# A three-pass float32 encoder layer: the two parts of h side by side for the up projection, and another order for its first and last products

## The chip, the cores and the metric

The kernel runs on one core of a Trainium2 chip. The metric is the device time of one execution in microseconds, as the median of several runs. One more execution was recorded by the profiler; every row in this text comes from that one. The engines are TensorE (PE; PEld is its weight load), VectorE (DVE), ScalarE (ACT), GpSimd (POOL) and SyncE (SP), which only issues DMAs.

## The reference, cut to what matters

One layer, 512 tokens by 2048 channels, float32: an attention and pooling part, then a gated feed-forward part with a convolution over three tokens between its two projections. The change is in the first projection of the second part.

```python
def reference(x, ...):
    ...                                             # attention, pooling, w_o, residual
    h = rms_norm(x, pre_ffn_g[l])                   # (512, 2048)
    up = causal_dwconv(h @ w_up[l], conv_w[l], conv_b[l])          # w_up: 2048 x 11264
    y = (gelu(up[..., :D_FF]) * up[..., D_FF:]) @ w_down[l]        # w_down: 5632 x 2048
    x = x + rms_norm(y, post_ffn_g[l])
    return x
```

## The kernel before

**Two parts for each number.** Every factor is split into a rounded high part and the low rest, by `split`: ACT writes the high part (line 136 or 139) and DVE the low one (line 137 or 140). A plain product is then three matmuls (`mm3`, lines 152 to 154): high by high, high by low, low by high. The contraction runs over blocks of 128 channels (`kb`), and the tokens are the columns that stream through TensorE.

**The transposed h.** h lies with its channels on the partitions in four tiles `gT` of [128, 2 parts, 4 blocks, 512 tokens]. So the high and the low part of one block are 2048 elements apart, and half of the tokens of one part are 256 neighbouring columns.

**The up projection.** Its weights have 88 blocks of 128 columns, in 22 units `u` of four: two for the gate, two for the value. The first three units (`PLAIN`) are plain: `w00` in two pieces by halves of the tokens (`gate_part`), then `w10` and four calls of `up`, each 16 blocks by 2 banks by 3 matmuls. The other 19 units are 38 pieces, k = 0 to 37, one per unit for the gate and one for the value, each computed with seven products instead of eight (Strassen's scheme in Winograd's form; "the sevens" below): the 2048 channels and the 512 tokens are cut in halves, and each of the products (k, i), i = 1 to 7, multiplies a sum of weight blocks by a sum of quarters of h. Four factors are quarters of `gT` themselves (i = 1, 7, 2, 4); three are sums that `h_sums` makes into the tiles `h5`, `h3`, `h6` of [128, 2 parts, 8 blocks, 256 tokens].

A product has eight blocks, and for each block two matmuls (`mm2`): the high weight against the high and low half together (2 x 256 = 512 columns, line 159), then the low weight against the high half (256 columns, line 161). We call them a pair.

```python
nc.tensor.matmul(ps.rearrange("p (a b) -> p a b", a=2), l[0], pair, start=first, stop=False, skip_group_check=onto)
nc.tensor.matmul(ps[:, :n], l[1], pair[:, 0, :], start=False, stop=last, skip_group_check=onto)
```

**Banks and sums.** Each piece k uses three PSUM banks: `a` for i = 1, 6, 7, 4 in this order, `g` for 5 and 3, `d` for 2. Between products that share a bank, its content is copied out by ACT (`keep`): `za` after 1 (line 1066), `zb` after 5 (line 1072), `zm` after 6 and 7 (lines 1076 and 1080), `z` after 4 (line 1090); DVE adds them up. `zb` has one buffer, which is read by the addition after 7 of the same k (line 1081).

**The weights of a product.** `Factors` loads raw blocks four to ten products ahead: `x` through SP (or `w` and `x` apart for the first and the last k, the set `alone`), `y` and `z`. POOL adds further blocks to them in memory by accumulating DMAs (line 1016), each after the split that used the sum so far: x is used by 1, then (+ one block) by 5, then by 6, then by 4. Raw `x` tiles are a ring of four. `make` splits the raw tile four products ahead, into a ring of four pairs `wfh` and `wfl`, so a split also waits until TensorE has finished the product four places earlier.

**What sets the order.** The order on TensorE is written out: `Factors.order` interleaves k with the rest of k - 1 (per k: (k,1), (k-1,6), (k,2), (k-1,7), (k,5), (k-1,4), (k,3)), with an explicit list for the last ten. On the other engines a scheduler orders the instructions by their program order and its estimates. After the sevens come the products `p` of the down projection, also by sevens (`multiply`, `mm3`); the first two are prepared inside the loop over the sevens by `next_first` (`ah`, `al` of the left factor; `bh`, `bl` of the right one, from raw `t`).

Of the kernel before, what the change touches and what calls it, by code (L numbers as in the profile page):

```python
# [76 lines left out]
def encoder_layer(ctx: ExitStack, tc: tile.TileContext, x, xT, vecs, rel, post_mix, post_ffn,  # L77
# [72 lines left out]

    def mm3(ps, l, r, first, last):
        nc.tensor.matmul(ps, l[0], r[0], start=first, stop=False)  # L152
        nc.tensor.matmul(ps, l[0], r[1], start=False, stop=False)  # L153
        nc.tensor.matmul(ps, l[1], r[0], start=False, stop=last)  # L154

    def mm2(ps, l, pair, first, last, onto):

        n = pair.shape[-1]
        nc.tensor.matmul(ps.rearrange("p (a b) -> p a b", a=2), l[0], pair, start=first, stop=False,  # L159
                         skip_group_check=onto)  # L160
        nc.tensor.matmul(ps[:, :n], l[1], pair[:, 0, :], start=False, stop=last, skip_group_check=onto)  # L161

    def new_pair(name, a, b):

# [411 lines left out]
    with tc.tile_pool(name="p2", bufs=1, reuse_waits="tile") as p2:  # L576
# [104 lines left out]
        def turn_back(t0, pair):  # L681

            ps = bank(f"xt{t0}_{pair}")
            for k in range(2):
                kb = 2 * pair + k
                for t in range(2):
                    nc.tensor.transpose(ps[:, k * T + t * P:k * T + (t + 1) * P],
                                        xn[t0 + t][:, kb * P:(kb + 1) * P], ident)
            for k in range(2):
                kb = 2 * pair + k  # L690
                split(*blk(hT, kb, slice(t0 * P, t0 * P + T)), ps[:, k * T:(k + 1) * T], col(V_PREFFN, kb))

        whole = slice(0, D // 2)
        for cc in range(2):
# [1 line left out]
        norm(0)  # L696
        for t in range(2):
            load_x(t, acc8(f"x{t}", "B"))
        hT = new_hT("gT")
        ps4 = wo_product(4, 0, a22)  # L700
        x2(0, y11, 0, whole)
        x2(0, y12, 1, whole)
# [17 lines left out]
        def gate_part(q, t0):  # L720
            sl = slice(t0 * P, t0 * P + T)
            for kb in range(4 * q, 4 * q + 4):
                for j in range(2):
                    mm3(ups[0][j][:, sl], part(gate_w[q], j, slice(kb % 4 * P, (kb % 4 + 1) * P)), blk(hT, kb, sl),
                        kb == 0, kb == KD - 1)

        for q in range(4):
# [11 lines left out]
        for q in range(4):  # L739
            w = weights.get(f"w10_{q}")  # L740
            for kb in range(4 * q, 4 * q + 4):
                for j in range(2):
                    mm3(ups[1][j], part(w, j, slice(kb % 4 * P, (kb % 4 + 1) * P)), blk(hT, kb),
                        kb == 0, kb == KD - 1)
        nc.vector.reduce_sum(total, ssq2, axis=AX.X)
        rstd(rt, total)
# [117 lines left out]
    with tc.tile_pool(name="p3", bufs=2, reuse_waits="tile") as p3:  # L864
# [38 lines left out]
        def up(u, p, between=()):  # L903
            ps = [bank(f"up{u}_{p}_{j}") for j in range(2)]
            between = list(between)
            for i in range(4):
                w = weights.get(f"w{p}{u}_{i}")
                factors.prefetch(4 - len(weights.specs) + weights.used)
                for kb in range(4 * i, 4 * i + 4):
                    for j in range(2):  # L910
                        mm3(ps[j], part(w, j, slice(kb % 4 * P, (kb % 4 + 1) * P)), blk(hT, kb),
                            kb == 0, kb == KD - 1)
                step = between.pop(0) if between else None
                if step:
                    step()
                next(sums_step, None)
            return ps
# [14 lines left out]


        T = S // 2
        hs = {i: sums_pool.tile([P, 2, 8, T], F32R, tag=f"h{i}", bufs=1, name=f"h{i}") for i in (5, 3, 6)}

        def quarter(k, t, i):

            return tuple(hT[2 * k + i][:, p, :, t * T:(t + 1) * T] for p in range(2))
# [12 lines left out]
        def h_sums(i):  # L952
            def whole(k, t):
                v = raw_x(f"q{k}{t}").rearrange("p (a b) -> p a b", a=4)
                hi, lo = quarter(k, t, i)
                nc.vector.tensor_add(v, f32(hi), f32(lo))
                return v

            def keep(n, v):
                hi, lo = (hs[n][:, p, 4 * i:4 * i + 4, :] for p in range(2))  # L960
# [12 lines left out]
            keep(3, a12)  # L973
# [6 lines left out]
        class Factors:  # L980
# [3 lines left out]
            def __init__(self):  # L984
                n = 2 * (NU - PLAIN)

                self.alone = 0, n - 1
                place_of = {1: 0, 6: 8, 2: 2, 7: 10, 5: 4, 4: 12, 3: 6}  # L990
                order = sorted((7 * k + at, k, i) for k in range(n) for i, at in place_of.items())
                end = [(n - 1, 1), (n - 2, 6), (n - 1, 5), (n - 2, 7), (n - 1, 3), (n - 1, 6), (n - 2, 4),
                       (n - 1, 7), (n - 1, 2), (n - 1, 4)]
                self.order = [(k, i) for _, k, i in order if (k, i) not in end] + end
                self.raw, self.made, self.loaded, self.used = {}, [], 0, 0

            def block(self, k, m, kh):
# [64 lines left out]
        def keep(k, i):  # L1062
# [5 lines left out]
                v = wide(zs[k, "1"])  # L1068
                nc.vector.tensor_add(v, banks.pop((k, "d")), v)
            elif i == 5:  # L1070
                zs[k, "5"] = pair_tile("zb", 1)
                nc.scalar.activation(wide(zs[k, "5"]), banks[k, "g"], AF.Copy)  # L1072
            elif i == 6:
                zs[k, "m"] = pair_tile("zm", 2)
                v = wide(zs[k, "m"][:, :1])
# [2 lines left out]
            elif i == 7:  # L1078
                v = wide(zs[k, "m"][:, 1:])
                nc.scalar.activation(v, banks[k, "a"], AF.Copy)  # L1080
                nc.vector.tensor_add(v, wide(zs.pop((k, "5"))), v)
            elif i == 4:
                keep_all(k)

# [14 lines left out]
        def seven(k, i):  # L1099
# [2 lines left out]
                banks[k, BANK[i]] = bank(f"q{BANK[i]}_{k}")  # L1102
            ps = banks[k, BANK[i]]
            for kb in range(8):
                mm2(ps, part(w, kb), h_factor(i, kb), i in FIRST and kb == 0, kb == 7, i not in FIRST)

        def first_left():

# [282 lines left out]
```

## Time and profile before

| | |
|---|---|
| plain runs | 1891.73, 1895.92, 1905.63 us (median 1895.92) |
| profiled execution | 1905.3 us, span from first to last instruction 1903.3 us |
| PE busy in the span | 1881.8 us (99%), 9438 matmuls |
| PEld, DVE, ACT, POOL busy | 1592.7, 1422.5, 981.8, 313.6 us |
| mean granted TensorE clock | 0.997 |
| first product of the sevens starts | 703.2 us |
| last product of the sevens starts | 1459.6 us |

Times in rows are microseconds from the start of the span; the second column of a timeline row is the duration, and a bracket at its end tells how long the engine was idle before and what released it. Matmuls overlap: the next one starts before the duration of the last is over, so the spacing of starts is what counts. In rows grouped by wait, the numbers are the total, the count and the longest.

### The profile page before, as it was taken

To read this page: it belongs to the slowest core of one execution; us is meant where nothing else is said; L and a number is where in the kernel's file an instruction comes from. 1 tells how busy PE (TensorE), PEld (TensorE's weight loads), DVE (VectorE), ACT (ScalarE), POOL (GpSimd) and SP (SyncE) were. 2 spreads that over 40 slices of the span, in tenths; PEclk is the share of its full clock that TensorE was granted. 3 is DMA by queue.
4 is the path that set the end of the run, shared out by engine and by line. 5 is a ranking of instruction groups with operands and counts; after the bars stand their busy time and mean duration, and the time that the engine had idled before them with its cause. 6 is when DMAs were issued, how large, how long until landed. Compare 5 with 4: busy or idle time off the path is not lost.

```text
span 1903.3 us, 24613 instructions
## 1 busy us (share of the span) xinstructions
PE 1881.8 (99%) x9438; PEld 1592.7 (84%) x9438; DVE 1422.5 (75%) x1616; ACT 981.8 (52%) x1238; POOL 313.6 (16%) x403
## 2 busy tenths in 40 slices
PE   9999999999999999999999999999998999999998
PEld 7888888888888888888888888888887788888886
DVE  5554345587698566888788887888877799998877
ACT  6333233346465345556555565555655665465543
POOL 4101011000000011221212212122120112222221
PEclk9999999999999999999999999999999999999999
DMA  7598399359796758888888888888886999999998
GB/s 247 164 258 226 96 282 222 98 173 316 245 313 197 204 161 198 197 198 198 199 204 199 198 197 199 204 199 197 200 179 193 350 271 244 248 221 236 225 226 238
DMA packets 188230, 410.24 MB, mean 216 GB/s; under 512 B 11536, under 2 KB 62608, under 8 KB 183568
## 3 DMA queue, kind: packets, MB, share of 16 engines
q0 software_dynamic: 56384, 155.21, 44.0%
q1 hardware_dynamic: 131728, 253.46, 38.7%
q8 instruction: 74, 1.21, 0.2%
q14 instruction: 44, 0.36, 0.1%
HBM read 352.00 MB, written 106.95 MB: 241 GB/s over the span
## 4 chain that ended last, share of the span: by engine, by line
PE 93%; DVE 2%; DMA 2%; issue 1%; ACT 1%; POOL 0%; SPq 0%; POOLq 0%; DVEq 0%; ACTq 0%
PE qa L159 14%; PE qg L159 7%; PE qa L161 7%; PE p L154 6%; PE p L152 6%; PE p L153 6%; PE qg L161 4%; PE qd L159 3%; PE m L152 3%; PE m L153 3%; PE m L154 3%; PE up L153 2%; PE up L154 2%; PE up L152 2%; PE qd L161 2%; PE u L152 2%
## 5 line engine op out<-in xcount | busy, mean ns | idle before, releaser
L159 PE MATMUL qa<-gT,wfh 128*128 128x512 f32 x912 | 327.6, 399 | 1.3 <-ACT zm L1076 1.0
L161 PE MATMUL qa<-gT,wfl 128*128 128x256 f32 x912 | 256.1, 281 | 0.0
L137 DVE TENSOR_TENSOR wfl<-wx,wfh 128x1024 fp32r<-128x1024 f32 x152 | 185.9, 1223 | 79.8 <-ACT wfh L136 79.8
L136 ACT ACTIVATE wfh<-wx 128x1024 fp32r<-128x1024 f32 x152 | 160.9, 1058 | 147.2 <-PE qa L159 88.1
L159 PE MATMUL qg<-h,wfh 128*128 128x512 f32 x608 | 218.5, 399 | 5.1 <-ACT zb L1072 5.1
L152 PE MATMUL p<-bh,ah 128*128 128x512 f32 x560 | 219.1, 391 | 1.5 <-ACT ah L136 1.5
L154 PE MATMUL p<-bh,al 128*128 128x512 f32 x560 | 219.3, 392 | 1.0 <-DVE al L137 1.0
L153 PE MATMUL p<-bl,ah 128*128 128x512 f32 x560 | 219.0, 391 | 1.3 <-DVE bl L137 1.3
L159 PEld LDWEIGHTS qa<-gT,wfh 128*128 128x128 f32 x912 | 171.4, 188 | 44.6 <-ACT zm L1076 1.3
L1016 POOL DMA_DIRECT2D wx<-in_w_up x114 | 97.9, 862 | 468.3 <-DVE wfl L137 454.7
L161 PEld LDWEIGHTS qa<-gT,wfl 128*128 128x128 f32 x912 | 172.3, 189 | 0.0
L161 PE MATMUL qg<-h,wfl 128*128 128x256 f32 x608 | 170.8, 281 | 0.0
L159 PEld LDWEIGHTS qg<-h,wfh 128*128 128x128 f32 x608 | 114.2, 188 | 34.2 <-ACT zb L1072 5.7
L136 ACT ACTIVATE bh<-b 128x2048 fp32r<-128x2048 f32 x56 | 106.9, 1917 | 63.4 <-DVE b L804 36.2
L137 DVE TENSOR_TENSOR bl<-b,bh 128x2048 fp32r<-128x2048 f32 x56 | 127.5, 2286 | 8.7 <-PE p L153 8.0
L136 ACT ACTIVATE wfh<-wy 128x1024 fp32r<-128x1024 f32 x76 | 80.7, 1061 | 101.9 <-PE qg L159 39.0
L154 PEld LDWEIGHTS p<-bh,al 128*128 128x128 f32 x560 | 105.8, 189 | 23.9 <-DVE al L137 1.8
L152 PEld LDWEIGHTS p<-bh,ah 128*128 128x128 f32 x560 | 105.9, 189 | 23.7 <-ACT ah L136 1.9
L153 PEld LDWEIGHTS p<-bl,ah 128*128 128x128 f32 x560 | 105.8, 189 | 23.6 <-DVE bl L137 1.6
L161 PEld LDWEIGHTS qg<-h,wfl 128*128 128x128 f32 x608 | 114.9, 189 | 0.0
L859 POOL DMA_DIRECT2D sum<-part x60 | 71.3, 1201 | 253.5 <-DVE part L850 115.6
L159 PE MATMUL qd<-gT,wfh 128*128 128x512 f32 x304 | 109.1, 399 | 0.0
(500 smaller groups left out, 4452.6 us busy)
## 6 DMA issues: line engine op xcount, KB each, us to landing
wx<-in_w_up POOLq DMA_DIRECT2D x114, 512.0 KB, 6.9
sum<-part POOLq DMA_DIRECT2D x70, 512.0 KB, 8.7
b<-in_w_down SPq DMA_DIRECT2D x32, 1024.0 KB, 9.5
wx<-in_w_up SPq DMA_DIRECT2D x40, 512.0 KB, 5.4
wz<-in_w_up SPq DMA_DIRECT2D x38, 512.0 KB, 6.1
wy<-in_w_up SPq DMA_DIRECT2D x38, 512.0 KB, 4.5
wy<-in_w_up POOLq DMA_DIRECT2D x38, 512.0 KB, 6.9
wt<-in_w_o POOLq DMA_DIRECT2D x16, 1024.0 KB, 11.9
```

Of the source, the lines that this page charges most:

```text
L136: rounded = nc.scalar.activation(hi, src, AF.Copy)
L137: nc.vector.tensor_sub(lo, src, f32(hi))
L152: nc.tensor.matmul(ps, l[0], r[0], start=first, stop=False)
L153: nc.tensor.matmul(ps, l[0], r[1], start=False, stop=False)
L154: nc.tensor.matmul(ps, l[1], r[0], start=False, stop=last)
L159: nc.tensor.matmul(ps.rearrange("p (a b) -> p a b", a=2), l[0], pair, start=first, stop=False, skip_group_check=onto)
L161: nc.tensor.matmul(ps[:, :n], l[1], pair[:, 0, :], start=False, stop=last, skip_group_check=onto)
L859: nc.gpsimd.dma_start(dest, v, accum_op=ALU.add)
L1016: nc.gpsimd.dma_start(self.raw[k, what], self.block(k, m, kh), accum_op=ALU.add)
```

## The change

h for the up projection gets another layout: per block of 128 channels one run of four pieces of 256 columns, low and high of the first half of the tokens, then high and low of the second half. Both parts of one half are then 512 neighbouring columns, and the high parts of both halves are so too (pieces 1 and 2). The sums `h5`, `h3`, `h6` get high and low side by side per block. The plain products of whole rows (`w10`, `up`) read the high part as one run of 512, and the low part as two runs of 256 (pieces 0 and 3). The tables for the first and the last products change, the copy `zb` of the last k takes a piece of the ring of `x`, and the second of the `next_first` calls comes after (36,4) instead of after (37,7).

```diff
     def mm3(ps, l, r, first, last):
         nc.tensor.matmul(ps, l[0], r[0], start=first, stop=False)
-        nc.tensor.matmul(ps, l[0], r[1], start=False, stop=False)
+        low = ps if len(r[1].shape) == 2 else ps.rearrange("p (a b) -> p a b", a=2)
+        nc.tensor.matmul(low, l[0], r[1], start=False, stop=False)
...
-    def mm2(ps, l, pair, first, last, onto):
-
-        n = pair.shape[-1]
-        nc.tensor.matmul(ps.rearrange("p (a b) -> p a b", a=2), l[0], pair, start=first, stop=False,
-                         skip_group_check=onto)
-        nc.tensor.matmul(ps[:, :n], l[1], pair[:, 0, :], start=False, stop=last, skip_group_check=onto)
+    def mm2(ps, l, pair, hi, first, last, onto):
+
+        n = pair.shape[-1] // 2
+        sl = slice(hi * n, (hi + 1) * n)
+        nc.tensor.matmul(ps, l[0], pair, start=first, stop=False, skip_group_check=onto)
+        nc.tensor.matmul(ps[:, sl], l[1], pair[:, sl], start=False, stop=last, skip_group_check=onto)
...
+    AT = (1, 0), (2, 3)
+
+    def new_gT():
+        return [big.tile([P, 4, 4, S // 2], F32R, tag="hT", bufs=4, name=f"gT{i}") for i in range(4)]
+
+    def g_half(gT, kb, t):
+        return tuple(gT[kb // 4][:, kb % 4, at, :] for at in AT[t])
+
+    def g_both(gT, kb):
+        v = gT[kb // 4][:, kb % 4]
+        return v[:, 1:3, :].rearrange("p a b -> p (a b)"), v[:, 0:4:3, :]
...
-                        mm3(ps[j], part(w, j, slice(kb % 4 * P, (kb % 4 + 1) * P)), blk(hT, kb),
+                        mm3(ps[j], part(w, j, slice(kb % 4 * P, (kb % 4 + 1) * P)), g_both(hT, kb),
...
-        hs = {i: sums_pool.tile([P, 2, 8, T], F32R, tag=f"h{i}", bufs=1, name=f"h{i}") for i in (5, 3, 6)}
+        hs = {i: sums_pool.tile([P, 8, 2, T], F32R, tag=f"h{i}", bufs=1, name=f"h{i}") for i in (5, 3, 6)}
...
             if i in hs:
-                return hs[i][:, :, kb, :]
+                return hs[i][:, kb].rearrange("p a b -> p (a b)"), 0
             k, t = {1: (0, 0), 7: (0, 1), 2: (1, 0), 4: (1, 1)}[i]
-            return hT[2 * k + kb // 4][:, :, kb % 4, t * T:(t + 1) * T]
+            return hT[2 * k + kb // 4][:, kb % 4, 2 * t:2 * t + 2].rearrange("p a b -> p (a b)"), 1 - t
...
+                begin = [(0, 1), (0, 5), (0, 2), (0, 3)]
+                end = [(n - 1, 5), (n - 2, 6), (n - 1, 3), (n - 1, 1), (n - 2, 7), (n - 1, 6), (n - 2, 4),
+                       (n - 1, 7), (n - 1, 2), (n - 1, 4)]
...
-                end = [(n - 1, 1), (n - 2, 6), (n - 1, 5), (n - 2, 7), (n - 1, 3), (n - 1, 6), (n - 2, 4),
-                       (n - 1, 7), (n - 1, 2), (n - 1, 4)]
...
-                zs[k, "5"] = pair_tile("zb", 1)
-                nc.scalar.activation(wide(zs[k, "5"]), banks[k, "g"], AF.Copy)
+                zs[k, "5"] = raw_x("zb")[:, :S] if k == end else wide(pair_tile("zb", 1))
+                nc.scalar.activation(zs[k, "5"], banks[k, "g"], AF.Copy)
...
-            if (k, i) in ((end, 6), (end, 7)):
+            if (k, i) in ((end, 6), (end - 1, 4)):
                 next_first()
```

The first products were (0,1), (0,2), (0,5), (0,3). What this does to the instructions on ACT is shown in three places. In the names, the number after `qa`, `qg` or `qd` is k and the last one counts buffers.

The first place is ACT's queue around the copy of the first (0,5). Before:

```order
L136 ACTIVATE wfh_5754<-wx_5615 128x1024
L1066 ACTIVATE za_5776<-qa_0_5759 128x512
L868 ACTIVATE cb_5745<-z_5737,vec_72 128x512
L136 ACTIVATE wfh_5780<-wx_5610 128x1024
L136 ACTIVATE wfh_5803<-wz_5617 128x1024
L1072 ACTIVATE zb_5824<-qg_0_5807 128x512
```

And now:

```order
L136 ACTIVATE wfh_5754<-wx_5615 128x1024
L1081 ACTIVATE za_5776<-qa_0_5759 128x512
L882 ACTIVATE cb_5745<-z_5737,vec_72 128x512
L136 ACTIVATE wfh_5780<-wx_5608 128x1024
L1087 ACTIVATE zb_5802<-qg_0_5785 128x512
L136 ACTIVATE wfh_5804<-wz_5617 128x1024
```

The copy `zb` has moved ahead of one split of weights; on TensorE (0,5) is now the second product and (0,2) the third.

The second place is ACT's queue near the end of the sevens, where the last k enters. Before:

```order
L136 ACTIVATE wfh_12290<-wy_12136 128x1024
L1066 ACTIVATE za_12312<-qa_37_12295 128x512
L868 ACTIVATE cb_12264<-z_12253,vec_72 128x512
L136 ACTIVATE wfh_12314<-wx_12089 128x1024
L1076 ACTIVATE zm_12335<-qa_36_12117 128x512
L136 ACTIVATE wfh_12338<-wx_11848 128x1024
L136 ACTIVATE wfh_12361<-wy_12136 128x1024
L1080 ACTIVATE zm_12335<-qa_36_12117 128x512
L1072 ACTIVATE zb_12359<-qg_37_12342 128x512
```

And now:

```order
L136 ACTIVATE wfh_12291<-wy_12004 128x1024
L1087 ACTIVATE zb_12312<-qg_37_12295 128x512
L882 ACTIVATE cb_12265<-z_12254,vec_72 128x512
L136 ACTIVATE wfh_12314<-wx_12029 128x1024
L1091 ACTIVATE zm_12335<-qa_36_12119 128x512
L136 ACTIVATE wfh_12338<-wx_11848 128x1024
L136 ACTIVATE wfh_12358<-wy_12090 128x1024
L1081 ACTIVATE za_12379<-qa_37_12362 128x512
```

The copy `zb` of k = 37 stood behind both copies `zm` of k = 36; now it stands ahead of them, and `za` of k = 37 has taken a later place.

The third place is ACT's queue some instructions on, where the first right factors of the down projection are split (`t` holds the raw ones). Before:

```order
L136 ACTIVATE ah_12438<-a_12436 128x1024
L1090 ACTIVATE z_12458<-qa_36_12117 128x256
L136 ACTIVATE bh_12432<-t1_12430 128x2048
L868 ACTIVATE ca_12464<-z_12458,vec_72 128x512 x2
L1080 ACTIVATE zm_12423<-qa_37_12295 128x512
L136 ACTIVATE bh_12492<-t1_12490 128x2048
```

And now:

```order
L136 ACTIVATE ah_12438<-a_12436 128x1024
L1105 ACTIVATE z_12458<-qa_36_12119 128x256
L136 ACTIVATE bh_12432<-t1_12430 128x2048
L882 ACTIVATE ca_12464<-z_12458,vec_72 128x512 x2
L136 ACTIVATE bh_12474<-t1_12472 128x2048
L1095 ACTIVATE zm_12423<-qa_37_12362 128x512
```

The second `bh` has moved ahead of the copy `zm` of (37,7), for which (37,4) waits on TensorE.

On SP the load of raw x for k = 37 takes the place that the load of w for k = 37 had, one period of k earlier, and on POOL its first accumulation moves with it.

More of the change, by code (lines that the diff above doesn't have):

```diff
@@ L698, in encoder_layer @@
             load_x(t, acc8(f"x{t}", "B"))
-        hT = new_hT("gT")
+        hT = new_gT()
         ps4 = wo_product(4, 0, a22)
@@ L723, in gate_part @@
                 for j in range(2):
-                    mm3(ups[0][j][:, sl], part(gate_w[q], j, slice(kb % 4 * P, (kb % 4 + 1) * P)), blk(hT, kb, sl),
+                    mm3(ups[0][j][:, sl], part(gate_w[q], j, slice(kb % 4 * P, (kb % 4 + 1) * P)), g_half(hT, kb, t0 // 2),
                         kb == 0, kb == KD - 1)
@@ L742, in encoder_layer @@
                 for j in range(2):
-                    mm3(ups[1][j], part(w, j, slice(kb % 4 * P, (kb % 4 + 1) * P)), blk(hT, kb),
+                    mm3(ups[1][j], part(w, j, slice(kb % 4 * P, (kb % 4 + 1) * P)), g_both(hT, kb),
                         kb == 0, kb == KD - 1)
@@ L959, in keep @@
             def keep(n, v):
-                hi, lo = (hs[n][:, p, 4 * i:4 * i + 4, :] for p in range(2))
+                hi, lo = (hs[n][:, 4 * i:4 * i + 4, p, :] for p in range(2))
                 split(hi, lo, v)
@@ L990, in __init__ @@
                 place_of = {1: 0, 6: 8, 2: 2, 7: 10, 5: 4, 4: 12, 3: 6}
+                begin = [(0, 1), (0, 5), (0, 2), (0, 3)]
+                end = [(n - 1, 5), (n - 2, 6), (n - 1, 3), (n - 1, 1), (n - 2, 7), (n - 1, 6), (n - 2, 4),
+                       (n - 1, 7), (n - 1, 2), (n - 1, 4)]
                 order = sorted((7 * k + at, k, i) for k in range(n) for i, at in place_of.items())
-                end = [(n - 1, 1), (n - 2, 6), (n - 1, 5), (n - 2, 7), (n - 1, 3), (n - 1, 6), (n - 2, 4),
-                       (n - 1, 7), (n - 1, 2), (n - 1, 4)]
-                self.order = [(k, i) for _, k, i in order if (k, i) not in end] + end
+                self.order = begin + [(k, i) for _, k, i in order if (k, i) not in begin + end] + end
                 self.raw, self.made, self.loaded, self.used = {}, [], 0, 0
@@ L1104, in seven @@
             for kb in range(8):
-                mm2(ps, part(w, kb), h_factor(i, kb), i in FIRST and kb == 0, kb == 7, i not in FIRST)
+                mm2(ps, part(w, kb), *h_factor(i, kb), i in FIRST and kb == 0, kb == 7, i not in FIRST)
         def first_left():
```

6 lines of the change are left out of this document (3 added, 3 removed).

## The prediction

> **What bounds the kernel now.** I read the page first, above all the chain that ended last.
>
> ```profile
> PE 93%; DVE 2%; DMA 2%; issue 1%; ACT 1%; POOL 0%; SPq 0%; POOLq 0%; DVEq 0%; ACTq 0%
> ```
>
> TensorE (PE) holds 93% of that chain, so two things can move the end: the spacing of its matmuls, and the few places where it stands. A matmul's own duration overlaps the next one, so I go by starts. The window of line 159 alone (the high matmul of each pair in the sevens; columns: stretch, length, PE busy and count, PEld busy and count, clock, DMA share, GB/s), and then the timeline of TensorE in four places:
>
> ```profile
> 740.00:1380.00 640.00, 640.00 (x1812) 340.32 (x1812) 1.00 0.86 199
> 719.81 0.40 PE L159 MATMUL qa<-h,wfh 128*128 128x512 f32 x1
> 720.05 0.28 PE L161 MATMUL qa<-h,wfl 128*128 128x256 f32 x1
> 720.17 0.40 PE L159 MATMUL qa<-h,wfh 128*128 128x512 f32 x1
> 595.98 0.39 PE L152 MATMUL up<-gT,w_0h 128*128 128x512 f32 x1
> 598.70 0.39 PE L152 MATMUL up<-gT,w_0h 128*128 128x512 f32 x1
> 593.67 0.28 PE L153 MATMUL up<-gT,w_3h 128*128 128x256 f32 x1
> 593.79 0.28 PE L154 MATMUL up<-gT,w_3l 128*128 128x256 f32 x1
> 593.91 0.40 PE L152 MATMUL up<-gT,w_0h 128*128 128x512 f32 x1
> 1891.70 0.39 PE L154 MATMUL yl<-wb,gl 128*128 128x512 f32 x1
> 1891.93 0.28 PE L152 MATMUL yl<-wb,gh 128*128 128x256 f32 x1
> ```
>
> A pair of the sevens takes 640/1812 = 0.3532 us, of which the 512 columns take about 0.236 (719.81 to 720.05) and the 256 about 0.118. The plain products, whose 512 columns lie in one run, need (598.70 - 595.98)/12 = 0.2267 us; 256 columns need 0.120, also when 512 follow (593.79 to 593.91), and 512 in front of 256 still 0.23 (1891.70 to 1891.93). So a pair of these two would cost 0.2267 + 0.120 = 0.3467 us. The extra 0.0065 us sits in the 512 columns of the sevens, which are read as two runs of 256, far apart.
>
> Then the standing times: the waits of TensorE, and the timeline around the longest.
>
> ```profile
> PE qg L159 <- ACT zb L1072: 5.1, 2, 3.6
> 711.55 0.28 PE L161 MATMUL qg<-h,wfl 128*128 128x256 f32 x1
> 713.35 0.51 PE L159 MATMUL qg<-h,wfh 128*128 128x512 f32 x1 [1.51 <-ACT zb L1072]
> 713.69 0.28 PE L161 MATMUL qg<-h,wfl 128*128 128x256 f32 x1
> 1417.17 0.28 PE L161 MATMUL qd<-gT,wfl 128*128 128x256 f32 x1
> 1418.45 0.51 PE L159 MATMUL qa<-gT,wfh 128*128 128x512 f32 x1 [1.01 <-ACT zm L1076]
> 1441.06 0.28 PE L161 MATMUL qa<-gT,wfl 128*128 128x256 f32 x1
> 1444.89 0.50 PE L159 MATMUL qg<-h,wfh 128*128 128x512 f32 x1 [3.55 <-ACT zb L1072]
> 1443.52 0.69 DVE L1081 TENSOR_TENSOR zm<-zb,zm 128x512 f32<-128x512 f32 x1
> 1444.24 0.60 ACT L1072 ACTIVATE zb<-qg 128x512 f32<-128x512 f32 x1 [1.41 <-DVE zm L1081]
> ```
>
> **Part 1, the pairs.** With high and low side by side the 512 columns of every first matmul are one run: 0.0065 us less per pair. Of the 266 products with 8 pairs I count the 263 up to (36,4), since what follows lies under VectorE (part 4): 263 x 8 x 0.0065 = **13.7 us less**. Bounds: nothing, if the two runs are not the cause; and, if 256 columns could cost half of 512 (0.1133), 2104 x (0.3532 - 0.3400) = 27.8. I take 13.7, since all four steps of it stand in rows.
>
> The Trainium skill, "SBUF — State Buffer", in the section on the DMA port swizzle, says that each access that leaves a 16-byte line pays, and that runs which hit a line at least twice are free. Runs of 256 floats are long by that rule, so by it a single jump costs nothing and this term is 0; the row of 0.236 against 0.2267 speaks for the jump. I go by the row and keep the rule's result as a rival.
>
> The other side: the plain products of w10 and of four `up` calls (5 x 32 = 160 low matmuls) now read their low half as two runs. Nearest row: the same form in the sevens, 0.0065 more each, **1.0 us more** (0 to 160 x 0.0132 = 2.1).
>
> **Part 2, the first products.** (0,3) follows (0,5) into the same bank and waits for its copy `zb`: 711.55 to 713.35 is 1.80 against 0.12, and the pair after it starts 0.34 apart against 0.236. Together 1.8 us. Now (0,2) with 2.8 us lies between, and the copy no longer stands behind the weights that this slot frees: **1.8 us less** (bound 0, were (0,5), now second, to lack its weights; this row shows their copy waiting for TensorE, not for a DMA):
>
> ```profile
> 697.74 1.06 ACT L136 ACTIVATE wfh<-wx 128x1024 fp32r<-128x1024 f32 x1 [3.43 <-PE up L153]
> ```
>
> **Part 3, the last products.** (37,3) waits 1441.06 to 1444.89: 3.83 - 0.12 + 0.10 = 3.8 us. The two rows behind it show why: `zb` has one buffer, which the addition of (36,7) has to read first. Now (37,5) writes a piece of the `x` ring, and (36,6) lies between it and (37,3): **3.8 us less** (bound 0). The ring's piece was freed by (35,4), long before.
>
> The stop at 1418.45 (1.16 + 0.11 = 1.3 us) is another thing: ACT was late because weights were late.
>
> ```profile
> 1377.72 0.33 SPq L1002 DMA_DIRECT2D wx<-in_w_up  x1
> 1397.39 0.33 SPq L1002 DMA_DIRECT2D wx<-in_w_up  x1
> 1404.22 2.63 POOL L1016 DMA_DIRECT2D wx<-in_w_up  x3 [2.70 <-DMA wx<-in_w_up]
> 1404.80 9.10 DMA wx<-in_w_up
> 1414.00 1.06 ACT L136 ACTIVATE wfh<-wx 128x1024 fp32r<-128x1024 f32 x1 [2.42 <-DMA wx<-in_w_up]
> ```
>
> The load of x for k = 37 goes out at 1397.39, and its own accumulation holds POOL's queue 2.70 us until it has landed; the two accumulations behind it go out with it and land after 9.10 us (a row of the chain). In the change this load takes the place of the one at 1377.72 and its accumulation stands behind that of y for k = 34 instead of k = 35: the same stop, one period earlier. I take **0** (1.3 less if the earlier landing clears the queue; 1.8 more if the loads still running there stretch the 9.1 us of that landing by as much).
>
> **Part 4, the turn to the products p.** From the end of (36,4), at 1453.5, VectorE sets the time.
>
> ```profile
> 1453.47 0.40 PE L159 MATMUL qa<-gT,wfh 128*128 128x512 f32 x1
> 1454.69 1.23 DVE L137 TENSOR_TENSOR al<-a,ah 128x1024 fp32r<-128x1024 f32 x1 [1.00 <-ACT ah L136]
> 1476.77 1.22 DVE L137 TENSOR_TENSOR al<-gc,ah 128x1024 fp32r<-128x1024 f32 x1
> 1475.15 0.49 PE L152 MATMUL p<-bh,ah 128*128 128x512 f32 x1 [1.53 <-ACT ah L136]
> 1476.90 0.56 PE L153 MATMUL p<-bl,ah 128*128 128x512 f32 x1 [1.26 <-DVE bl L137]
> 1478.04 0.79 PE L154 MATMUL p<-bh,al 128*128 128x512 f32 x1 [0.58 <-DVE al L137]
> 1484.12 0.39 PE L153 MATMUL p<-bl,ah 128*128 128x512 f32 x1
> 1454.82 1.91 ACT L136 ACTIVATE bh<-t 128x2048 fp32r<-128x2048 f32 x1
> 1444.00:1454.00 10.00, 9.11 (x51) 7.94 (x52) 3.94 (x5) 3.61 (x5) 0.00 (x0) 1.00 0.75 234
> 1474.00:1484.00 10.00, 7.01 (x16) 5.08 (x17) 6.28 (x4) 6.63 (x8) 1.99 (x3) 0.66 1.02 426
> ```
>
> The first row is the start of (37,7). From the one `al` to the other VectorE works almost without a break, with ACT's `cb` between: 24.5 us from 1453.5 to the matmul at 1478.04, whatever TensorE does meanwhile. The change puts the second `bh` (1.9 us) ahead of the copy of (37,7) on ACT, so (37,4) starts up to 1.9 us later against (36,4) than now, and TensorE reaches the third p later by as much. It stood 1.53 + 1.26 + 0.58 = 3.4 us there: **0**, and 1.9 more without that cover. What this takes away is standing, and the standing had a price: the granted clock fell (0.66 over the stretch; 1.00 is full), and the 14 steps from 1478.04 to 1484.12 took 6.08 us instead of 14 x 0.2267 = 3.17, 2.9 us. With the first of the three gaps gone I expect the clock to hold, and 0.5 of the 2.9 to come back as a wait for the next `al`: **2.4 us less** (0 to 2.9). For it speaks that 3.55 us of idleness just before 1444.89 left the clock at 1.00.
>
> The Trainium skill, "TensorE: Matmul & The Clock Gate", Part 1, has the gate look at windows of about 3.4 us that run free and halve the clock after an idle one: by it the sum is the same, and which case comes depends on how the window falls.
>
> **Sum.** -13.7 + 1.0 - 1.8 - 3.8 + 0 - 2.4 = -20.7 us. The profiled execution took 1905.3 us (span 1903.3), so 1884.6 there. It was as long as the longest of the three plain runs; against their median, 1895.9, the same difference gives **1875.2 us**, 1.1% less.
>
> **Rivals.** *The clock falls all the same*: everything else as above, -18.3, 1877.6 us. For it: two gaps of about 1.3 and 0.6 us remain before the third p. *The two runs are not what costs* (the change's main edit does nothing): terms 13.7 and 1.0 vanish, -8.0, 1887.9 us. For it: no other matmul with two runs is in this trace; against it: widths of 512 and 256 alternate elsewhere without loss. *The weights can't follow*: a k period falls from 19.8 to 19.4 us, and POOL's accumulations become the bound of the sevens, giving the 13.7 back: -7.0, 1888.9 us. Against it: DMA share 0.86, and ACT's waits between 740 and 1390, of which the longest group stands below, are for TensorE and none for a DMA. *Slower: the 160 low matmuls in two runs drop to another rate*, since input and output are both cut there. The transposes below show one: 1.03/8 = 0.13 us for 128 columns at most, 1.0 ns a column against 0.2267/512 = 0.44: 160 x 512 x 0.56 ns = 46 us, 1921 us. It decides from 21/160 = 0.13 us each; against it, the sevens read two runs at 0.236.
>
> ```profile
> ACT wfh L136 <- PE qg L159: 76.7, 56, 1.5
> 587.00 1.03 PE L687 MATMUL xt<-ident,x 128*128 128x128 f32 x8
> ```
>
> **Chances.** Forecast 0.52, clock 0.25, two runs 0.13, weights 0.05, slower 0.05. A run tells about 1% (19 us) from no change. A fifth of the forecast falls short of that and a third of the clock's case reaches it: faster 0.50, within 1% 0.45, slower 0.05. The range must hold the second and third rival and, below, part of the larger bound of part 1: 1867 to 1892 us.
>
> **What would show it.** The pair in the window: 0.347 us (0.353 kills part 1); 0.233 instead of 0.227 at every third plain matmul of `up`; no wait for `zb` anywhere; one stop of 1 to 2 us some 20 us before the old 1418; clock 1.00 through the turn. Wrong if TensorE waits for weights in the middle of the sevens, or if `up` grows by more than 3 us.

## The result and the profile after

The change takes 1898.54 us (median of 12 runs, 1895.54 to 1902.21), the kernel before 1897.9 us in the same comparison (12 runs, 1891.73 to 1908.45): ratio 0.9995, 95% interval 0.9976 to 1.0013. No difference, where 1875.2 us were forecast, and outside the range.

The two traces do not say "no difference". The profiled execution of the change took 1898.3 us (span 1896.4), that of the kernel before 1905.3 (span 1903.3). The same matmul, counted from the start of the program, begins at these times (us; worked out from the starts in both traces):

```
matmul     before      after    difference
 3300       703.54     704.01     +0.47     first product of the sevens
 3600       758.33     757.01     -1.32
 7200      1394.33    1393.01     -1.32
 7500      1452.41    1447.73     -4.68
 7800      1526.09    1518.64     -7.45     in the products p
 last      1894.68    1887.23     -7.45
```

So in the traces 7.9 us are gained at three places, and nothing between 758 and 1394, where part 1 wanted its 13.7. The view that answers to the prediction's window is that of line 161, now the long matmul of each pair (columns as there: stretch, length, PE busy and count, PEld, clock, DMA share, GB/s); below it a window of all matmuls of `up`, first of the change, then of the kernel before:

```profile
740.00:1380.00 640.00, 640.00 (x1813) 340.42 (x1812) 1.00 0.87 199
```

```profile
640.00:700.00 60.00, 60.00 (x266) 49.73 (x265) 3.94 (x6) 1.00 0.60 167
```

```profile
640.00:700.00 60.00, 60.00 (x266) 49.70 (x265) 3.94 (x6) 1.00 0.58 172
```

The same number of pairs in the same 640 us: 0.3533 us a pair, as before, with all 512 columns in one run. And in `up`, whose low matmuls now read two runs, 266 matmuls in 60 us as before. So the two runs cost nothing at either place.

The stops in the change, by the waits of TensorE (total, count, longest), by the timeline (rows of ACT and of the matmuls that waited; other rows between them left out), and by windows of all engines around them (the third number from the end is the clock):

```profile
PE qa L161 <- ACT zm L1095: 2.1, 1, 2.1
PE qa L161 <- ACT zm L1091: 1.5, 1, 1.5
PE p L154 <- DVE bl L137: 1.3, 1, 1.3
PE p L155 <- DVE al L137: 1.0, 2, 0.6
```

```profile
1396.21 1.06 ACT L136 ACTIVATE wfh<-wx 128x1024 fp32r<-128x1024 f32 x1 [1.45 <-DMA wx<-in_w_up]
1397.81 0.50 PE L161 MATMUL qa<-gT,wfh 128*128 128x512 f32 x1 [1.45 <-ACT zm L1091]
1456.72 0.50 PE L161 MATMUL qa<-gT,wfh 128*128 128x512 f32 x1 [2.12 <-ACT zm L1095]
1472.22 0.51 PE L154 MATMUL p<-bl,ah 128*128 128x512 f32 x1 [1.25 <-DVE bl L137]
1473.36 0.50 PE L155 MATMUL p<-bh,al 128*128 128x512 f32 x1 [0.63 <-DVE al L137]
```

```profile
1454.00:1462.00 8.00, 5.88 (x31) 4.79 (x30) 8.00 (x11) 4.11 (x5) 0.00 (x0) 1.00 0.25 59
1470.00:1484.00 14.00, 12.12 (x53) 9.45 (x52) 11.60 (x9) 7.92 (x9) 2.72 (x4) 1.00 1.01 424
```

No wait for `zb` is left. One stop stands 20.6 us ahead of the old 1418, for weights that come late (ACT waits for a DMA, the copy `zm` stands behind it). The stop ahead of (37,4) has grown from 0.32 us of idleness to 2.12. This was its row in the kernel before:

```profile
1459.60 0.50 PE L159 MATMUL qa<-gT,wfh 128*128 128x512 f32 x1 [0.32 <-ACT zm L1080]
```

One of the three stops in the turn is gone, and the clock stays at 1.00 through both places. Of all that the prediction wanted to see, the first two things are missing, and both belong to the price of the two runs: 0.347 us for the pair, and 0.233 instead of 0.227 at every third plain matmul of `up`.

### The profile page after: what moved, and what is told of

Its sections match the earlier page's. It is cut to its first block, busy times and chain, and to the rows that moved or that the text cites. A ratio compares the mean times of both kernels' runs of the same rounds, so it can differ in the third digit from the quotient of the medians.

```text
span 1896.4 us, 24608 instructions
## 1 busy us (share of the span) xinstructions
PE 1877.9 (99%) x9438; PEld 1590.4 (84%) x9438; DVE 1422.1 (75%) x1616; ACT 981.7 (52%) x1238; POOL 313.8 (17%) x403
## 4 chain that ended last, share of the span: by engine, by line
PE 92%; DVE 3%; issue 2%; ACT 1%; DMA 1%; POOL 0%; SPq 0%; POOLq 0%; DVEq 0%; ACTq 0%
PE qa L161 14%; PE qg L161 7%; PE qa L162 7%; PE p L155 6%; PE p L154 6%; PE p L152 6%; PE qg L162 4%; PE qd L161 3%; PE m L155 3%; PE m L154 3%; PE m L152 3%; PE up L154 2%; PE up L155 2%; PE up L152 2%; PE qd L162 2%
```

## The experiments

Each comparison has its own runs of the kernel before, on several chips. These runs are spread much wider than those of the change: most lie between 1903 and 1911 us, and some, the shorter group, between 1891 and 1900, with few between. In the comparison above 7 of 12 lay below 1900; in the later ones 4 of 19, 1 of 10, 1 of 17, 1 of 15 and 2 of 13. The granted clock of these runs does not tell the groups apart: in the five later comparisons its mean is 0.996 for the nine runs below 1900 us and 0.996 for the 53 above 1903. So there were two questions: why the pair did not change, and what the two groups are.

**The kernel before again.** 

> The kernel before, unchanged, for a second profiled execution. Theory A (the first profiled execution, 1905.3 us, met more stops than a usual one, so the 7.4 us by which the two traces differ are not a difference of medians): this one is nearer to the median of 1897.9 us, and at least one of the stops of the first (713.35: 1.8 us, 1444.89: 3.8 us, the low clock after 1478: 2.9 us) is smaller or missing by 2 us or more in sum. Theory B (the stops are the same in every execution, and what is gained there in the changed kernel is lost elsewhere): the same three stops return within 0.5 us each, and the time is within 2 us of 1905.

Measured: 1907.74 us, all three stops as in the first trace (1.7, 4.1, and 1.7 + 1.5 + 0.9 us in the turn). Only the clock differs: it already fell behind the stop near 1445 (0.83 over 1440 to 1460, against 1.00 in the first trace), and again in the turn (0.85 over 1484 to 1490). Theory A fell for this execution: it belongs to the longer group too. Its time is 0.7 us beyond the 2 us that theory B allowed.

**The pair by itself.** A block of series ahead of the kernel's work; the core of it:

```diff
+    def series(name, units, times, banks=1, runs=1):
+        ps = [bank(f"{name}{i}") for i in range(banks)]
+        ...
+            nc.tensor.matmul(b, data[:, 896:], r, start=k < banks, stop=k >= len(todo) - banks, ...)
+    series("pair", [512, 256], 24)
+    series("apart", [512, 256], 24, banks=2)
+    series("jump", [512, 256], 24, runs=2)
+    series("twos", [512, 512, 256, 256], 12)
+    ...
```

> The changed kernel with eleven series of matmuls on zeros ahead of its work, each into banks that nobody reads: widths 512; 256; 512 and 256 in turn into one bank; the same into two banks; the same with the 512 columns in two runs; two 512 and two 256 in turn; four and four; 512 and 384; 512 and 128; two 512 and one 256; 384. Theory A (the turn of widths is what costs): 512 alone 0.2267 us, 256 alone 0.120; a pair 0.3533 in one bank, in two banks and with two runs alike; two and two 0.3467 or 0.350 a pair, four and four 0.3467 or 0.348. Theory B (the short matmul adds onto columns that the long one has just written): 0.3467 a pair in two banks, 0.3533 in one. Theory C (something of the stretch of the sevens, as its transfers or its weights): 0.3467 a pair in every series here. Theory D (two runs cost): 0.3467 a pair in one run, 0.3533 in two; the trace of the change speaks against it.

The timeline of three series, 48 matmuls each (start, duration of the group; the fourth row tells where the third series ends):

```profile
22.70 8.64 PE L143 MATMUL pair<-data 128*128 128x512 f32 x48
31.18 8.64 PE L143 MATMUL apart<-data 128*128 128x512 f32 x48
39.66 8.64 PE L143 MATMUL jump<-data 128*128 128x512 f32 x48
48.14 2.02 PE L143 MATMUL twos<-data 128*128 128x512 f32 x10
```

From start to start 8.48 us for 24 pairs: 0.3533 us in one bank, in two banks, and with the 512 columns in two runs. 512 alone took 0.2267, 256 alone 0.1200; two and two 0.3483 a pair, four and four 0.3508, 512 with 384 0.4133 in its second half (0.2267 + 0.1733, for 384 alone, would be 0.4000). So the extra comes with the turn of widths; neither the bank nor the runs nor the transfers of the sevens have a part in it (theories B, C and D fall).

**Long ones first.** Eight long matmuls, then the eight short ones of a product; and two and two:

```diff
             for kb in range(8):
-                mm2(ps, part(w, kb), *h_factor(i, kb), ...)
+                long2(ps, part(w, kb), *h_factor(i, kb), ...)
+            for kb in range(8):
+                short2(ps, part(w, kb), *h_factor(i, kb), ...)
```

> The changed kernel, where each product of the sevens does its eight long matmuls (512 columns) first and its eight short ones (256) after them. Theory A (the turn of widths costs 0.0065 us a pair): 8 x (0.2267 + 0.120) = 2.773 us a product instead of 2.827, 263 products: 14.0 us less, near 1884.5 us, ratio to the kernel before 0.993, unless weights that come too late take part of it back. Theory B (the short matmul adds onto columns just written): the same 14 us. Theory C (something of the stretch of the sevens): 2.827 us a product, no difference, ratio 1.000. The low part of a weight is needed 1.8 us later in a product than before, so a stop for VectorE should get shorter, not longer.

> The changed kernel, where the products of the sevens take two blocks at a time: two long matmuls (512 columns), then two short ones (256). In the series measured by themselves two and two took 0.3483 us a pair, a pair in turn 0.3533, four and four 0.3508; eight and eight cost 2.792 us a product in the kernel. Theory A (each turn of width costs what the series shows): 8 x 0.3483 = 2.787 us a product instead of 2.827, 266 products: 10.6 us less than the change, near 1888 us, ratio to the kernel before 0.990 to 0.995. Theory B (a fixed price for each turn, 0.0065 us for one up and one down): half of it back, 0.350 a pair, 7 us less.

Measured: 1889.24 us, ratio 0.9928 (0.9905 to 0.9951), and 1887.6 us, ratio 0.9903 (0.9885 to 0.9922). The windows of the long matmul, eight and eight above, two and two below:

```profile
740.00:1380.00 640.00, 459.02 (x1834) 329.77 (x1835) 1.00 0.88 201
```

```profile
740.00:1380.00 640.00, 576.99 (x1839) 279.69 (x1838) 1.00 0.89 201
```

640/1834 x 8 = 2.792 us a product and 640/1839 x 8 = 2.784, as the series by themselves have it (2.787 for two and two, as theory A says). Both kernels take less time than either the change or the kernel before, by less than 1%, and TensorE has no wait in these windows: weights keep up. Eight and eight takes 9.3 us less than the median of the change where theory A said 14: one turn in 16 matmuls costs 0.018 us, nearly three times what one turn in two costs.

**One half of the change at a time.** The new layout with the old tables, and the new tables with the old layout:

> The changed kernel with the old tables for the first and last products, the old buffer of zb and the old place of the second call of next_first: only the layout of h is new. Theory A (the layout changes nothing, the order all that the traces show): the stops near 713 (1.8 us) and 1445 (3.8 us) and the low clock after 1478 are back in the trace; if they cost in an ordinary run what they cost in the profiled one, the ratio to the kernel before is 1.000 and the time 6 to 8 us over that of the change; if they do not, both are the same as before within 0.2%. Theory B (the layout costs something that the traces hide, as much as the order gains): slower than the kernel before by 5 to 8 us, ratio 1.003 to 1.004.

> The kernel before with the new tables, the copy zb of the last k in the ring of x and the new place of the second call of next_first; the layout of h is the old one. Single runs of the kernel before, and of the new layout with the old tables, lie in two groups, 1892 to 1900 and 1903 to 1909 us, and those of the change between 1895 and 1903. Theory A (the order alone makes that difference, the layout none): as the change, all runs between 1893 and 1904 us, median within 3 us of 1898.5, the stop near 1398 of 1.5 to 2.2 us, no stop near 713 or 1445, clock 1.00 through the turn. Theory B (it takes the layout for it): two groups 10 us or more apart, as before.

Layout alone: 12 runs in two groups (1892.95 to 1898.04, five; 1905.96 to 1908.00, seven), ratio 0.9995 (0.9971 to 1.0019); its trace has the stops of the kernel before. Order alone: 1900.92 us (1896.36 to 1901.85), ratio 0.9962 (0.9949 to 0.9976), one group. So the layout does nothing, and the order gains. That it also takes away the shorter group fits its one group, but in that comparison the kernel before had only 1 of 10 runs there; the stronger sign is the first comparison, with 7 of 12 for the kernel before and none for the change. The last products alone:

> The kernel before with the new table for the last products and the copy zb of the last k in the ring of x; the first products, the place of the second call of next_first and the layout are the old ones. Theory A (the wait of 3.8 us near 1445 and what follows it in the turn make the two groups): one group of times, between 1895 and 1904 us, 1.8 us over the kernel with the whole new order, whose stop of 1.8 us near 713 is back. Theory B (the place of the second call of next_first makes them): two groups 10 us or more apart.

Measured: 1902.0 us (12 runs, 1900.51 to 1903.27), ratio 0.9977 (0.9968 to 0.9987), the stop near 713 back, and that near 1445 gone. One group, but the kernel before had only one run below 1900 beside it, so this does not tell what makes the groups.

**In search of the shorter group.** Three more executions of the kernel before, and both kernels twice in one launch:

> The kernel before again, to see an execution of its shorter group (below 1900 us). If it is one: theory A (the stops of the sevens and of the turn are what comes and goes) has them shorter by 8 us or more in sum; theory B (the spacing of the pairs comes and goes) has 0.347 to 0.350 us a pair instead of 0.3533; theory C (it lies outside, in the first 100 us or after the last matmul) has 8 us or more of the difference there. If it is one of the longer group: the stops are those of the first two traces within 1 us.

> The kernel before again, with the same three theories as for the one ahead of it.

> The kernel before again, with the same three theories as for the two ahead of it.

> The kernel before, its whole computation done twice in one launch, the second time with the same result. So one trace holds a first and a second pass. Times near 3800 us. Theory A (the longer group of 1903 to 1909 us belongs to a pass that comes first after something else, the shorter of 1892 to 1900 to a warm one): the second pass has stops at the end of the sevens and in the turn that are 8 us or more shorter than in the first (in sum 14 us there). Theory B (the groups are drawn anew for each execution by something at the end of the sevens): the totals lie in three groups 10 to 13 us apart, and the two passes of the trace need not differ. Theory C (the groups come from outside the sevens): the stops are the same in both passes, whatever the totals.

> The changed kernel, its computation done twice in one launch. Theory A (its order takes away the longer group, and a warm pass has little to gain): the second pass has stops near those of the first (1.7 us one period before the old place, 2.4 us ahead of (37,4), 2.9 us in the turn) within 2 us in sum, and the total is equal to that of the kernel before done twice where that is in its shorter group, 8 us or more less for each pass of the longer group. Theory B (the layout costs in a warm pass): the second pass is longer than that of the kernel before by 3 us or more at places that the order does not touch.

Measured: 1905.9, 1904.65 and 1905.74 us; none below 1900. Twice: 3811.08 us (3809.51 to 3812.17) before, 3791.75 us (3786.87 to 3794.64) for the change: 9.7 us less for each pass. The second passes have the stops of the first, so theory A of the kernel done twice, that a warm pass is the shorter one, fell.

But in these traces the pair has *two* lengths. Two of them are shown here (the third has the shorter one for 62 pairs behind its stop near 1418, and the second pass of the kernel before done twice for 390 pairs behind a hitch of 0.1 us). First the windows of the long matmul in one of them (before_3), then its timeline at the stop between, then the windows in the other (before_4):

```profile
740.00:1140.00 400.00, 400.00 (x1133) 212.72 (x1133) 1.00 0.87 200
1190.00:1380.00 190.00, 190.00 (x548) 102.64 (x549) 1.00 0.88 203
```

```profile
1183.10 1.05 ACT L136 ACTIVATE wfh<-wy 128x1024 fp32r<-128x1024 f32 x1
1183.25 0.19 PEld L159 LDWEIGHTS qa<-gT,wfh 128*128 128x128 f32 x1 [0.45 <-ACT zm L1076]
1183.25 0.50 PE L159 MATMUL qa<-gT,wfh 128*128 128x512 f32 x1
```

```profile
714.00:820.00 106.00, 106.00 (x307) 57.32 (x306) 1.00 0.88 203
830.00:1400.00 570.00, 570.00 (x1614) 303.13 (x1614) 1.00 0.88 199
```

400/1133 = 0.353 us a pair up to a stop of 0.3 us at 1183.25, and 190/548 = 0.347 after it, with the same instructions. In the other trace the wait for `zb` near 713 put the pairs at 106/307 = 0.345 by this count (310 pairs with 0.3467 from start to start), and a stop at 822.6 put them back. There are two rhythms, 0.3533 and 0.3467 us, which is exactly the sum of 0.2267 and 0.1200. A stop of TensorE may change from one to the other, and between stops a rhythm lasts. In nine passes with the stop near 713 (counting those with the old tables) it led to the short rhythm once. If it lasts through the 1990 pairs up to the next stop near 1418, it saves 1990 x 0.00667 = 13.3 us: 1905.3 - 13.3 = 1892.0, the lower edge of the shorter group. This was theory B of the three executions.

**What sets the rhythm.** A new comparison of the change, and a second block of series, with one or two matmuls of other widths ahead of the pairs:

> The changed kernel, unchanged, in a new comparison with the kernel before. The pairs of the sevens run in one of two rhythms, 0.3533 or 0.3467 us, and each stop of TensorE may change it: the trace of one more execution of the kernel before changed to 0.3467 at its stop near 713 and back at 823, another changed near 1184. Theory A (the change gains 8 to 10 us by its order in every execution, and loses the stop near 713 at which the kernel before gets the short rhythm in some of its executions, worth up to 13 us): the ratio goes with the share of such executions in the kernel before; where most of its runs lie at 1905 to 1909 us it is 0.995 to 0.996, with no run of the change below 1892. Theory B (the change gives nothing in ordinary runs): ratio 0.998 to 1.002 again, whatever the runs of the kernel before.

> The changed kernel with two groups of series on zeros ahead of its work. First eleven series of 16 matmuls of 512 columns, then nothing or one or two of another width (64 to 448), then 24 pairs of 512 and 256. Then 30 series of 12 pairs, each after a stop of TensorE for a copy by ACT, with nothing or one or two other widths ahead of the pairs, six of each kind. Theory A (what comes just ahead of the pairs sets their rhythm, without a stop too): at least one width gives 0.3467 us a pair and the others 0.3533, the same each time; after stops the same kind gives the same rhythm six times. Theory B (only a stop sets it, and by chance): all eleven 0.3533, and of the series after stops some of each kind 0.3467, some 0.3533.

The change: 1898.11 us (11 runs, 1895.06 to 1901.77), the kernel before 1907.43 (15 runs, one below 1900): ratio 0.9955 (0.9942 to 0.9967), as theory A has it. The series, with the mean of the last 18 pairs (ns), worked out from the starts:

```
ahead of the pairs     first steps from there on              a pair
(nothing)              227 113 233 117 241 120 236            353.3
256                    114 232 118 241 120 235 114            353.3
320                    143 233 117 231 113 232 118            346.7
384                    171 231 117 234 117 241 120            353.3
128, 128               57 113 285 118 231 112 233             346.7
64; 128; 192; 448; 256, 256; 384, 384                         353.3
```

After a stop, six times each: nothing ahead 0 of 6 in the short rhythm, 512 and 512 2, 256 2, 128 4, 384 5. So without a stop what comes just ahead decides, as far as one series of each kind can show it. After a stop the same kind gives now the one, now the other; that what comes ahead shifts the odds is only suggested by six series each. Both theories hold a part.

**The rhythm set on purpose.** One added matmul, whose result the next one overwrites:

```diff
             ps = banks[k, BANK[i]]
+            if (k, i) == (0, 1):
+                nc.tensor.matmul(ps[:, :320], part(w, 0)[0], h_factor(i, 0)[0][:, :320], start=True, stop=True, ...)
```

> The changed kernel with one more matmul ahead of the first product of the sevens: 320 columns into the bank that this product then begins anew, so the result is the same. In the series measured by themselves one matmul of 320 columns after a run of 512 put the pairs that followed into the short rhythm, 0.3467 us, and one of 256 or 384 did not. Theory A (the rhythm is what part 1 took for the price of the two runs, and what the kernel before has in its shorter group): 0.3467 us a pair from the start to the stop near 1396, 1959 x 0.00667 = 13.1 us less, 0.15 us more for the added matmul: near 1885.5 us, ratio 0.9885 where the kernel before has mostly the long rhythm. Theory B (in the kernel the rhythm is set by something else, its semaphores or transfers): 0.3533, and 0.15 us over the change.

> The same with 256 instead of 320 columns. Theory A: 0.3533 us a pair as in the change, 0.12 us over it, near 1898.5 us, ratio 0.995 to 0.996 against the kernel before where that has mostly the long rhythm. Theory B (any added matmul there helps): as with 320 columns.

With 320: 1892.48 us (6 runs, 1887.23 to 1895.14), ratio 0.9923 (0.9904 to 0.9941). With 256: 1897.34 us (1896.63 to 1899.29), ratio 0.9957 (0.9944 to 0.9970), no different from the change. The windows of the long matmul with 320, the timeline at the place between, and the window with 256:

```profile
740.00:1140.00 400.00, 400.00 (x1155) 216.37 (x1154) 1.00 0.89 202
1190.00:1380.00 190.00, 190.00 (x539) 101.03 (x538) 1.00 0.86 198
```

```profile
1152.63 0.28 PE L162 MATMUL qd<-gT,wfl 128*128 128x256 f32 x1
1152.85 0.50 PE L161 MATMUL qa<-gT,wfh 128*128 128x512 f32 x1
1153.18 0.28 PE L162 MATMUL qa<-gT,wfl 128*128 128x256 f32 x1
```

```profile
740.00:1380.00 640.00, 640.00 (x1812) 340.34 (x1812) 1.00 0.88 199
```

400/1155 = 0.346 us a pair from the added matmul on, until a hitch of 0.1 us at 1152.85 (0.22 instead of 0.12, behind a late `zm`) put it back to 190/539 = 0.353. So that execution kept 8.6 of the 13.1 us up to the end of these pairs. It is only 3.7 us shorter than the profiled execution of the change: its sevens began 2.6 us later, and the stop for late weights grew (2.36 us of idleness at 1392.92, and a clock of 0.50 over 1394 to 1396), which took another 2.4 us. The shortest, 1887.23, is near the 1885.5 that the whole would give.

## Why the prediction missed

**Part 1 failed, at the step that gave the extra 0.0065 us of the pair to the two runs.** The 0.2267 and 0.120 were right, and 0.3467 is a spacing that this pair really has. But the first row that it was compared with (719.81 to 720.05 in the sevens, two runs, followed by 256) differed from the plain products in two things, the runs and the turn of widths, and I picked the one that the change was about. The one argument against the other, that 512 and 256 stand beside each other elsewhere without loss, rested on single turns (593.79 to 593.91, 1891.70 to 1891.93), not on many in a row. The rival *two runs are not what costs* was right in its mechanism: with 512 columns in one run or two a pair took 0.3533 us, in the kernel and in the series. By the Trainium skill, "SBUF — State Buffer", the section on the DMA port swizzle, runs that use more than one element of a 16-byte line are free. For one jump in 512 columns the traces agree: 266 matmuls of `up` in 60 us, with and without two runs. What costs is the turn of widths, in the rhythm in which the pairs start. The 1.0 us for the 160 low matmuls of `up` fell with it: 0, the lower bound.

**Parts 2 to 4 held in these two traces.** Part 2: 1.79 us for 1.8 (the step from +0.47 to -1.32). Part 3: the wait of 3.8 us is gone, and the other stop came one period earlier, as said, at 1.7 us for 1.3, inside the bounds given: 3.36 us together for 3.8. Part 4: (37,4) starts 1.8 us later against (36,4) and TensorE stands as much less in the turn; the clock held; 2.77 us for 2.4. Together 7.92 us for the 8.0 that the sum has without part 1.

**The clock in part 4 was luck in part.** The prediction argued from 3.55 us of idleness ahead of 1444.89 that left the clock at 1.00. In the four other traces of the kernel before, and with the layout alone, the same stop has 0.83 to 0.91 over 1440 to 1460. Nor did the clock hold everywhere behind the stop ahead of (37,4): it has 1.00 in both traces of the change, but 0.83 over ten us there in both passes of the change done twice. The gain as a whole stands in every pair of traces: from matmul 7200 to 7800 the five traces of the kernel before take 131.4 to 132.9 us and the two of the change 125.6 and 126.0, which is 5.5 to 7.3 us for the 6.2 of parts 3 and 4. With the order alone, where the clock fell behind both stops (0.79 and 0.86), it is smaller: 128.1 us.

In the Trainium skill, "TensorE: Matmul & The Clock Gate", Part 1, the gate's windows run free, so that the outcome depends on how one falls. The traces agree: 3.55 us of idleness left the clock at 1.00 in the first trace, and the order alone stands only 2.37 us at 1399.23 and has 0.79 over the eight us around it:

```profile
1399.23 0.50 PE L159 MATMUL qa<-gT,wfh 128*128 128x512 f32 x1 [2.37 <-ACT zm L1077]
1396.00:1404.00 8.00, 5.63 (x24) 4.60 (x23) 6.17 (x9) 2.87 (x5) 3.17 (x4) 0.79 0.77 203
```

**The last step failed too, the move from the profiled execution to the median.** 1905.3 - 8.0 = 1897.3 us, and the change takes 1898. Instead I took the difference from 1895.9, the median of three runs, as if it were the same execution with a little noise. Six traced executions of the kernel before or of its order (five of the kernel, one with the new layout) all took 1904.65 to 1907.74 us, and the two runs of 1891.73 and 1895.92 were, by all that is shown here, something else. What they had was worth as much as all of parts 2 to 4 or more: so in a comparison where the kernel before had 7 of 12 runs below 1900 the ratio is 0.9995, and where it had 1 of 15 it is 0.9955.

**What part 2 could not see.** The wait near 713 was a cost of 1.8 us and at the same time a throw of the dice on the rhythm of the 1990 pairs behind it. Where it falls well and lasts, it would save 13.3 us; runs between the groups would fit a rhythm that changes on the way. The change takes the stop away, and after `up` the pairs start in the long rhythm in every one of the 16 traced passes that have these pairs and no added matmul. So, if the shorter group is the short rhythm, the change loses the bad runs and the good ones: its 23 runs lie between 1895.06 and 1902.21.

Open: no execution of the kernel before below 1900 us was traced. That the shorter group is the short rhythm rests on its size, on the change of rhythm at that stop in one trace and at other stops in this and three more, and on the added matmul that makes it on purpose; the group itself was not seen. Why the share of shorter runs differs so much between the comparisons (7 of 12, 1 of 15) wasn't found, nor what in TensorE keeps the two rhythms.

## What to carry to other kernels

When one row differs from its comparison in two ways, look for a row that differs in one, before the difference gets a price. When the plain runs of a kernel spread wider than its stops can explain, the profiled execution is one draw: predict from its own time, and ask what the others have. And where matmuls of 512 and 256 columns take turns, try them two and two: here that took 1887.6 us, 0.9903 of the kernel before, and its four runs lie within 1.5 us. Other widths were not tried so in the kernel.

## What the hardware did that was not expected

- 512 and 256 columns in turn run at 0.3533 or 0.3467 us a pair, each steady for hundreds of pairs (steps 241, 120, 236, 113, 233, 117 ns, or 233, 117, 231, 113). One matmul of 320 columns ahead of them gives the short one, 256 or 384 the long one; a stop of 0.1 to 0.3 us is enough to change it (1152.85, 1183.25).
- Two and two cost 0.3483 us a pair and four and four 0.3508 in the series, eight and eight 0.3490 in the kernel: fewer turns are not always cheaper.
- 512 and 384 in turn cost 0.4133 us a pair instead of 0.4000, 512 and 128 0.340.
- The same stop of 3.6 to 4.0 us has a granted clock of 1.00 over the 20 us around it in one trace and 0.83 to 0.91 in five.
